# The early sums of a gate-and-up group, made once instead of three times

## The chip, the cores and the metric

The kernel runs on one core of a Trainium2 chip. The metric is the time of one execution on the device in microseconds (us). Lower is better. The engines named below are TensorE (PE, the matmuls, with PEld for its weight loads), VectorE (DVE), ScalarE (ACT), GpSimd (POOL) and SyncE (SP, which issues the weight transfers). Each engine works through its own list of instructions in order and waits on semaphores where an instruction needs another engine's result.

## The reference

The reference is a two-block network in float32 on one sequence of 256 tokens of width 2048. Block one has an attention and retention mixer, a cross attention and a gated feed-forward layer; block two has another mixer and another feed-forward layer. The change touches only the feed-forward layer of block one, with 5632 hidden columns:

```
hf = rmsnorm(x, norm_ffn_g[l])
x = x + (jax.nn.silu(hf @ w_gate[l]) * (hf @ w_up[l])) @ w_down[l]
```

## The kernel before

Every float32 matrix is split into a high and a low part, and a product is made of three matmuls (`mm3`, L193 to L195: high by high, high by low, low by high). The weights stream in from memory as tiles of 128 x 2048 (1 MB each), in the order in which they are used. For each piece of a weight tile, ACT makes the high part by a cast (L175, `wh`) and DVE the low part by a subtraction (L176, `wl`). `half` (L319) hands out the next piece and prepares pieces ahead, so that up to five are in line.

The gate and up weights are computed together in 11 groups of 512 hidden columns, in three parts of 4, 4 and 3 groups (`PARTS`). Behind each part comes its share of the down product. One group is a call of `gemm_q` (L410). It runs 8 passes `u` over the inner dimension, each with 256 rows of the gate weight and 256 of the up weight, for 256 tokens. `KINDS = "NSNSNSNN"` says how each pass is done:

- "S" (passes 1, 3 and 5) is a Strassen step of seven products in place of eight. It needs sums of weight blocks, which DVE makes (L305, L309 and L310, `wt`), and has four pieces "a", "c", "b", "d".
- "N" (passes 0, 2, 4, 6 and 7) is a plain step of eight products with two pieces. The first piece gives two products into M2 and two into M4, the second two into M5 and two into M3.

The products gather in seven accumulators, M1 to M7, of one PSUM bank each. M2 to M5 come from a pool of four banks (`pg` in the profile), M1, M6 and M7 from another pool of four (`pp`). Only "S" passes add to M1, M6 and M7, so these three are complete behind pass 5; M2 to M5 are complete only in pass 7. Since all four `pg` banks are in use, the next group's product into a bank can't begin before the bank's old content has been read.

How the accumulators become gate and up: the early sums are a copy m of M1 (L844, ACT), u2 = M6 + m (L845, DVE) and u3 = M7 + u2 (L846, DVE). They are made by the function `early`, which `gemm_q` calls as `sums_done` at the end of a pass (L448) if no "S" pass is left. That holds behind passes 5, 6 and 7. The second and third call write the same values into the same tiles again. The rest is made when `gemm_q` returns:

- gate, first 128 tokens: M2 + m (L853, DVE, reads M2 for the last time), then silu (L854, ACT)
- gate, last 128 tokens: M4 + u3 (L855, DVE, reads M4 for the last time), then silu (L856, ACT)
- up: M5 + u2 and M5 + u3 (L857 and L858), M3 + that u2 (L859), and the two products with the gate (L861, L860), all on DVE

The order of the instructions on each engine is not written by hand. The framework plans it ahead of the run from a simulated timeline (`schedule_with_timeline_sim=True`), allots the buffers of the pools and puts the semaphores in. An instruction may therefore stand before others that were written earlier: DVE's list mixes weight pieces of the next group with the sums of the present one.

Of the kernel before, what the change touches and what calls it, by code (L numbers as in the profile page):

```python
# [17 lines left out]
S = 256  # L18
# [28 lines left out]
def tile_kernel(ctx, tc, x, xT, mem, memT, par, alibi, rdecay, ident_d, bc_rows, gm_wsT,  # L47
# [98 lines left out]
    def gps():  # L146
        return psg.tile([P, 512], F32, tag="g", name=nm("pg"))

    def sps():
        return pss.tile([P, 512], F32, tag="p", name=nm("pp"))  # L150
# [40 lines left out]
    def mm3(out, lh, rh, start, stop):  # L191

        T.matmul(out, lhsT=lh[0], rhs=rh[0], start=start, stop=False)  # L193
        T.matmul(out, lhsT=lh[0], rhs=rh[1], start=False, stop=False)  # L194
        T.matmul(out, lhsT=lh[1], rhs=rh[0], start=False, stop=stop)  # L195
# [68 lines left out]
    def kind(w, u):  # L264
        return KINDS[u] if w is w_gu else "N"
# [53 lines left out]
    def half(w, g, u, i, n):  # L319
        while pos[1] < len(pieces) and len(feed) < 1 + LOOKAHEAD:  # L320
            push()
        w_, g_, u_, i_, hi, lo = feed.pop(0)
        assert w_ is w and (g_, u_, i_) == (g, u, i)
        if isinstance(hi, list):
            return hi, lo
        return [[t[:, k * n:(k + 1) * n] for k in range(t.shape[-1] // n)] for t in (hi, lo)]
# [4 lines left out]
    def tick():  # L331
        for g in list(bg):
            try:
                next(g)
            except StopIteration:
                bg.remove(g)
# [8 lines left out]
    def need(lst, i):  # L345
        while lst[i] is None:
            assert bg
            tick()
        return lst[i]
# [60 lines left out]
    def gemm_q(wap, g, acts, sums_done):  # L410

        M = [None] * 8
        n = len(acts)
        ks = [kind(wap, u) for u in range(n)]
        total = {m: sum(1 if k == "S" else 2 if m in (2, 3, 4, 5) else 0 for k in ks) for m in range(1, 8)}
        done = [0] * 8

        def prod(m, a, b):  # L420
            if M[m] is None:
                M[m] = gps() if m in (2, 3, 4, 5) else sps()
            done[m] += 1
            mm3(M[m], a, b, done[m] == 1, done[m] == total[m])

        for u in range(n):
            a = need(acts, u)
            if ks[u] == "N":
                plan = [(0, [(2, 0, 0, 0), (2, 0, 1, 1), (4, 1, 0, 0), (4, 1, 1, 1)]),
                        (1, [(5, 1, 1, 0), (5, 1, 0, 1), (3, "D", 1, 0), (3, "D", 0, 1)])]  # L430
                for i, ops in plan:
                    hi, lo = half(wap, g, u, i, 512)
                    for m, t, k, b in ops:
                        prod(m, a.diff(k) if t == "D" else a.blk(k, t), (hi[b], lo[b]))
                    tick()
            else:
                plan = [("a", [(1, a.blk(0, 0), 0), (2, a.blk(1, 0), 1)]),
                        ("c", [(3, a.sums(3), 0)]),
                        ("b", [(5, a.sums(0), 0), (7, a.sums(2), 1)]),
                        ("d", [(6, a.sums(1), 0), (4, a.blk(1, 1), 1)])]  # L440
                for i, ops in plan:
                    hi, lo = half(wap, g, u, i, 512)
                    for m, x, b in ops:
                        prod(m, x, (hi[b], lo[b]))
                    if i in "cd":
                        tick()
            if "S" not in ks[u + 1:]:
                sums_done(M)  # L448
        return M

    def evac_fm(ps, r):
# [386 lines left out]
    for g0, g1 in PARTS:  # L838
        acts = [None] * (2 * (g1 - g0))
        for g in range(g0, g1):  # L840
            m, u2, u3 = flat(ft()), flat(ft()), flat(ft())

            def early(M):
                A.copy(m, M[1])  # L844
                V.tensor_tensor(u2, M[6], m, ALU.add)  # L845
                V.tensor_tensor(u3, M[7], u2, ALU.add)  # L846

            M = gemm_q(w_gu, g, hf_a, early)
            if g == 0:
                rsf[0] = sqf.rstd(D)  # L850
            r = [rsf[0][:, t:t + 1] for t in range(2)]
            s = [flat(ft()), flat(ft())]
            V.tensor_tensor(s[0], M[2], m, ALU.add)  # L853
            A.activation(s[0], s[0], AF.Silu, scale=r[0])  # L854
            V.tensor_tensor(s[1], M[4], u3, ALU.add)  # L855
            A.activation(s[1], s[1], AF.Silu, scale=r[1])  # L856
            V.tensor_tensor(u2, M[5], u2, ALU.add)  # L857
            V.tensor_tensor(u3, M[5], u3, ALU.add)  # L858
            V.tensor_tensor(u2, M[3], u2, ALU.add)  # L859
            V.scalar_tensor_tensor(s[0], u2, r[0], s[0], ALU.mult, ALU.mult)  # L860
            V.scalar_tensor_tensor(s[1], u3, r[1], s[1], ALU.mult, ALU.mult)  # L861
            spawn(ffn_pairs(s, acts, 2 * (g - g0)))
        for g in range(4):
            add_x(gemm_tm(w_down, g, acts, g0), g)
            if g1 == PARTS[-1][1]:
                spawn(next_in(g, h2_a, sq_f, gg, second_norm), 1)
# [218 lines left out]
    for g in range(2):  # L1085
        ps = gemm_tm(w_in2_t, g, h2_a)
        u = []
# [161 lines left out]
```

## Time and profile before

| | us |
|---|---|
| runs, median of 3 (lowest to highest) | 2601.64 (2598.96 to 2602.27) |
| the profiled execution | 2601.45 |
| its span, first to last instruction | 2599.7 |
| gate-and-up groups of part 1 (0 to 3) | about 807 to 962 of the span |
| part 2 (4 to 7) | about 1046 to 1224 |
| part 3 (8 to 10) | about 1308 to 1442 |

Each of the three stretches is followed by a down stage. A row of a group of instructions gives line, engine, operation, tiles (output from inputs, buffer numbers left out), shapes and count, then the busy time in us and the mean of one in ns, then the engine's idle time just before them and what ended it. A row of single instructions gives the start in us from the start of the span, the duration, and in brackets the idle time before it with the instruction that ended it. A row of waits gives who waited for whom: us in total, times, longest. A row of a stretch gives its bounds, its length, the busy time of PE, PEld, DVE, ACT and POOL with instruction counts, the granted clock of PE as a share of full speed, the share of the DMA engines that was busy, and GB/s. A duration on DVE or ACT overlaps the next instruction's by some 0.08 us, so what an instruction takes from a full queue is the step from its start to the next start.

### The profile page before, as it was taken

To read this page: it belongs to the slowest core of one execution; us is meant where nothing else is said; L and a number is where in the kernel's file an instruction comes from. 1 tells how busy PE (TensorE), PEld (TensorE's weight loads), DVE (VectorE), ACT (ScalarE), POOL (GpSimd) and SP (SyncE) were. 2 spreads that over 40 slices of the span, in tenths; PEclk is the share of its full clock that TensorE was granted. 3 is DMA by queue.
4 is the path that set the end of the run, shared out by engine and by line. 5 is a ranking of instruction groups with operands and counts; after the bars stand their busy time and mean duration, and the time that the engine had idled before them with its cause. 6 is when DMAs were issued, how large, how long until landed. Compare 5 with 4: busy or idle time off the path is not lost.

```text
span 2599.7 us, 32474 instructions
## 1 busy us (share of the span) xinstructions
PE 2567.3 (99%) x12823; PEld 2172.7 (84%) x12823; DVE 1789.2 (69%) x2284; ACT 1381.7 (53%) x1882; POOL 39.0 (2%) x41
## 2 busy tenths in 40 slices
PE   8999999999999999999999999999999999999998
PEld 7888888888887878878887888888888888888887
DVE  7666566556579885888588767866777745777754
ACT  6555554454466553555355555755555534555543
POOL 1000010000000000000000000000000000000000
PEclk9999999999999999999999999999999999999999
DMA  7455555554454555455555555555555555555563
GB/s 257 162 179 211 201 201 189 194 178 162 146 188 168 196 193 194 178 206 196 193 182 180 205 208 192 178 192 181 188 185 193 184 193 192 194 185 188 189 213 132
DMA packets 72727, 490.58 MB, mean 189 GB/s; under 512 B 8192, under 2 KB 8320, under 8 KB 14592
## 3 DMA queue, kind: packets, MB, share of 16 engines
q1 hardware_dynamic: 72576, 488.52, 53.1%
q8 instruction: 100, 1.64, 0.2%
q14 instruction: 51, 0.42, 0.0%
HBM read 486.39 MB, written 2.10 MB: 188 GB/s over the span
## 4 chain that ended last, share of the span: by engine, by line
PE 94%; DVE 3%; issue 1%; ACT 1%; DMA 0%; SPq 0%; POOL 0%; ACTq 0%; POOLq 0%; DVEq 0%
PE pg L362 24%; PE pg L193 17%; PE pg L195 17%; PE pg L194 17%; PE pg L366 12%; PE pp L193 2%; PE pp L195 2%; PE pp L194 2%; DVE wl L176 1%; PE pp L186 1%; ACT wh L175 1%; DVE wt L305 0%; DVE f L845 0%; DVE f L846 0%; DMA w<-in_w_in_f_dram 0%
## 5 line engine op out<-in xcount | busy, mean ns | idle before, releaser
L176 DVE TENSOR_TENSOR wl<-w,wh 128x1024 fp32r<-128x1024 f32 x866 | 1059.6, 1225 | 665.7 <-ACT wh L175 662.0
L175 ACT CAST wh<-w 128x1024 fp32r<-128x1024 f32 x866 | 909.2, 1051 | 863.9 <-PE pg L195 583.9
L193 PE MATMUL pg<-wh,r 128*128 128x512 f32 x2059 | 798.6, 392 | 12.7 <-DVE f L855 11.2
L194 PE MATMUL pg<-wl,r 128*128 128x512 f32 x2059 | 804.6, 391 | 0.0
L195 PE MATMUL pg<-wh,r 128*128 128x512 f32 x2059 | 802.3, 390 | 0.0
L362 PE MATMUL pg<-r,wh 128*128 128x512 f32 x2688 | 714.9, 395 | 11.4 <-ACT wh L175 7.0
L362 PEld LDWEIGHTS pg<-r,wh 128*128 128x128 f32 x2688 | 471.0, 189 | 86.2 <-ACT wh L175 7.0
L193 PEld LDWEIGHTS pg<-wh,r 128*128 128x128 f32 x2059 | 387.2, 188 | 98.3 <-DVE f L855 14.7
L195 PEld LDWEIGHTS pg<-wh,r 128*128 128x128 f32 x2059 | 387.6, 188 | 80.7
L194 PEld LDWEIGHTS pg<-wl,r 128*128 128x128 f32 x2059 | 387.8, 188 | 80.4 <-DVE wl L176 1.1
L366 PEld LDWEIGHTS pg<-r,wl 128*128 128x128 f32 x2688 | 391.2, 190 | 41.7
L366 PE MATMUL pg<-r,wl 128*128 128x256 f32 x2688 | 406.0, 282 | 0.0
L454 ACT COPY f<-pg 128x256 f32<-128x256 f32 x168 | 60.7, 374 | 88.7 <-PE pg L362 88.7
L175 ACT CAST wh<-wt 128x1024 fp32r<-128x1024 f32 x66 | 69.6, 1055 | 55.3 <-DVE wt L310 21.2
L455 DVE TENSOR_TENSOR f<-pg,f 128x256 f32<-128x256 f32 x168 | 68.9, 420 | 43.7 <-ACT f L454 43.7
L176 DVE TENSOR_TENSOR wl<-wt,wh 128x1024 fp32r<-128x1024 f32 x66 | 80.3, 1219 | 11.9 <-ACT wh L175 11.2
L1112 DVE SCALAR_TENSOR_TENSOR f<-f,pr,f 128x255 f32<-128x255 f32 x192 | 79.9, 479 | 0.0
L456 DVE TENSOR_TENSOR f<-f,rows 128x512 f32<-128x512 f32 x84 | 58.1, 692 | 3.4 <-ACT rows L231 0.8
L1109 ACT ACTIVATE f<-f,pr 128x256 f32<-128x256 f32 x96 | 52.6, 594 | 12.6 <-DVE f L456 12.5
L175 ACT CAST r<-f 128x512 fp32r<-128x512 f32 (+1 forms) x72 | 43.0, 598 | 13.7 <-DVE f L456 8.7
L193 PE MATMUL pp<-wh,r 128*128 128x512 f32 x127 | 49.6, 395 | 0.0
L195 PE MATMUL pp<-wh,r 128*128 128x512 f32 x127 | 49.5, 390 | 0.0
(192 smaller groups left out, 1354.0 us busy)
## 6 DMA issues: line engine op xcount, KB each, us to landing
w<-in_w_up_dram SPq DMA_DIRECT2D x96, 1024.0 KB, 4.7
w<-in_w_down_dram SPq DMA_DIRECT2D x92, 1024.0 KB, 4.7
w<-in_w_gu_dram SPq DMA_DIRECT2D x88, 1024.0 KB, 4.8
w<-in_w_in_t_dram SPq DMA_DIRECT2D x40, 1024.0 KB, 4.8
w<-in_w_in_f_dram SPq DMA_DIRECT2D x39, 1024.0 KB, 4.7
w<-in_w_o_dram SPq DMA_DIRECT2D x16, 1024.0 KB, 4.8
w<-in_w_xk_dram SPq DMA_DIRECT2D x16, 1024.0 KB, 4.8
w<-in_w_xv_dram SPq DMA_DIRECT2D x16, 1024.0 KB, 4.7
```

Of the source, the lines that this page charges most:

```text
L175: A.copy(hi, src)
L176: V.tensor_tensor(lo, src, hi.bitcast(F32), ALU.subtract)
L193: T.matmul(out, lhsT=lh[0], rhs=rh[0], start=start, stop=False)
L194: T.matmul(out, lhsT=lh[0], rhs=rh[1], start=False, stop=False)
L195: T.matmul(out, lhsT=lh[1], rhs=rh[0], start=False, stop=stop)
L362: T.matmul(ps[m], lhsT=hi[k][:, m * P:(m + 1) * P], rhs=ops[k].both(k % 2), start=begin and k == 0, stop=stop, skip_group_check=True)
L366: T.matmul(ps[m][:, S:], lhsT=lo[k][:, m * P:(m + 1) * P], rhs=ops[k].hi(k % 2), start=False, stop=False, skip_group_check=True)
L454: A.copy(f[:, m, :], ps[m][:, S:])
L455: V.tensor_tensor(f[:, m, :], ps[m][:, 0:S], f[:, m, :], ALU.add)
L456: V.tensor_tensor(f, f, bc2(need(r, 0)), ALU.mult)
L1109: A.activation(y[:, j, :], z[:, j, :], AF.Identity, scale=col("ffn_conv_w_2", 192 + c), bias=col("ffn_conv_b_2", c))
L1112: V.scalar_tensor_tensor(y[:, j, d:], z[:, j, :S - d], col("ffn_conv_w_2", 96 * (2 - d) + c), y[:, j, d:], ALU.mult, ALU.add)
```

## The change

The test for "is an S pass left" and the call move by one level of indentation, into the branch for "S" passes. Behind pass 5 the early sums are made as before; behind passes 6 and 7 ("N") nothing is made.

```
@@ -444,8 +444,8 @@
                         prod(m, x, (hi[b], lo[b]))
                     if i in "cd":
                         tick()
-            if "S" not in ks[u + 1:]:
-                sums_done(M)
+                if "S" not in ks[u + 1:]:
+                    sums_done(M)
         return M
```

`early`, `gemm_q`'s products, the final sums and everything else stay as they are.

More of the change, by code (lines that the diff above doesn't have):

```diff
@@ L446, in gemm_q @@
                         tick()
-            if "S" not in ks[u + 1:]:
-                sums_done(M)
+                if "S" not in ks[u + 1:]:
+                    sums_done(M)
         return M
```

## The prediction

> **What bounds the kernel now.** I read the head of the page first, then the waits of TensorE in the gate-and-up stage, then the stage's stretches, then single instructions around the group boundaries.
>
> ```profile
> span 2599.7 us, 32474 instructions
> PE 2567.3 (99%) x12823; PEld 2172.7 (84%) x12823; DVE 1789.2 (69%) x2284; ACT 1381.7 (53%) x1882; POOL 39.0 (2%) x41
> PE 94%; DVE 3%; issue 1%; ACT 1%; DMA 0%; SPq 0%; POOL 0%; ACTq 0%; POOLq 0%; DVEq 0%
> ```
>
> TensorE (PE) is busy for 2567.3 of 2599.7 us. The whole kernel can give back at most 32.4 us of idle PE, plus whatever PE loses while it counts as busy. The chain that ended last has 3% on VectorE (DVE), about 78 us; the question is whether the removed work is part of that. The waits of PE between 800 and 1450 us, which is gate, up and down, are two rows (total, times, longest):
>
> ```profile
> PE pg L193 <- DVE f L855: 11.2, 4, 3.1
> PE pg L193 <- ACT wh L175: 1.3, 4, 0.3
> ```
>
> Four times PE waits for L855, 2.8 us each. L855 is the addition `M4 + u3`: it releases M4's bank, which the next group's third product needs, and it needs `u3`, which the removed calls rewrite. By stretches (length, then busy time of PE, PEld, DVE, ACT, POOL, then granted clock and DMA):
>
> ```profile
> 807.00:962.00 155.00, 148.80 (x657) 121.53 (x656) 138.14 (x165) 87.29 (x101) 0.00 (x0) 0.99 0.54 191
> 962.00:1046.00 84.00, 84.00 (x376) 69.65 (x375) 46.38 (x45) 35.38 (x36) 0.00 (x0) 1.00 0.57 198
> 1046.00:1224.00 178.00, 174.55 (x775) 142.27 (x774) 157.77 (x180) 99.56 (x113) 0.00 (x0) 1.00 0.53 190
> 1308.00:1442.00 134.00, 130.95 (x569) 106.88 (x569) 115.19 (x131) 74.38 (x84) 0.00 (x0) 0.97 0.52 183
> ```
>
> The first, third and fourth are the gate-and-up groups of the three parts, the second a down stage. In the groups DVE is busy 86 to 89% of the time, in the down stage 55%, where PE is never idle. So DVE's 69% over the span hides a stage where it is nearly full, and PE's idle time is there. Now one boundary on DVE (start, duration; the first row ends the first call of the early sums, the second begins the second):
>
> ```profile
> 902.90 0.68 DVE L846 TENSOR_TENSOR f<-pp,f 128x512 f32<-128x512 f32 x1
> ...
> 904.64 0.68 DVE L845 TENSOR_TENSOR f<-pp,f 128x512 f32<-128x512 f32 x1
> 905.24 1.21 DVE L305 TENSOR_TENSOR wt<-w 128x1024 f32<-128x1024 f32 x1
> ...
> 906.97 0.68 DVE L846 TENSOR_TENSOR f<-pp,f 128x512 f32<-128x512 f32 x1
> 907.57 1.21 DVE L176 TENSOR_TENSOR wl<-w,wh 128x1024 fp32r<-128x1024 f32 x1
> ...
> 910.44 0.68 DVE L853 TENSOR_TENSOR f<-pg,f 128x512 f32<-128x512 f32 x1
> 911.04 0.68 DVE L845 TENSOR_TENSOR f<-pp,f 128x512 f32<-128x512 f32 x1
> 911.64 0.68 DVE L310 TENSOR_TENSOR wt<-wt,w 128x512 f32<-128x512 f32 x1
> 912.24 1.22 DVE L176 TENSOR_TENSOR wl<-wt,wh 128x1024 fp32r<-128x1024 f32 x1
> 913.38 0.68 DVE L846 TENSOR_TENSOR f<-pp,f 128x512 f32<-128x512 f32 x1
> 913.98 1.21 DVE L176 TENSOR_TENSOR wl<-wt,wh 128x1024 fp32r<-128x1024 f32 x1
> 915.11 1.22 DVE L305 TENSOR_TENSOR wt<-w 128x1024 f32<-128x1024 f32 x1
> 916.25 0.68 DVE L855 TENSOR_TENSOR f<-pg,f 128x512 f32<-128x512 f32 x1
> ```
>
> From 904.64 on no row shows idle time: DVE works through its queue without a pause for 12 us, and four of these instructions, the second and third calls, are what the change removes. PE at the same moment:
>
> ```profile
> 913.65 0.39 PE L194 MATMUL pg<-wl,r 128*128 128x512 f32 x1
> 913.88 0.39 PE L195 MATMUL pg<-wh,r 128*128 128x512 f32 x1
> 916.98 0.50 PE L193 MATMUL pg<-wh,r 128*128 128x512 f32 x1 [2.71 <-DVE f L855]
> ```
>
> Matmuls follow at 0.23 us, so the next was due at 914.11 and came at 916.98. Before the stall the new group had run its two products into M2.
>
> **The change, part by part.** The rows of the three lines over the whole run:
>
> ```profile
> L844 ACT COPY f<-pp 128x512 f32<-128x512 f32 x33 | 19.1, 577 | 0.1
> L845 DVE TENSOR_TENSOR f<-pp,f 128x512 f32<-128x512 f32 x33 | 22.6, 684 | 1.0 <-PE pp L195 0.7
> L846 DVE TENSOR_TENSOR f<-pp,f 128x512 f32<-128x512 f32 x33 | 22.5, 683 | 0.0
> ```
>
> 33 is three for each of 11 groups; one is left. (That the change leaves the repeats in place can't be: the call now stands in the branch for "S", and only pass 5 has no "S" behind it.) Removed are 22 copies of 0.58 us on ScalarE (ACT), 12.7 us, and 44 additions on DVE. Their occupancy is the step from start to start, 904.64 to 905.24, 0.60 us: 26.4 us of DVE, 2.40 us per group.
>
> *The four long stalls.* If the order on DVE stays and the queue closes up, L855 starts at 916.25 - 2.40 = 913.85. PE resumed 0.73 us behind L855's start, so at 914.58 against 914.11 due: 0.47 us late instead of 2.87. That needs the weight halves from ACT in time:
>
> ```profile
> 909.55 1.06 ACT L175 CAST wh<-wt 128x1024 fp32r<-128x1024 f32 x1 [1.66 <-PE pg L195]
> 911.16 0.73 ACT L854 ACTIVATE f<-f,s 128x512 f32<-128x512 f32 x1 [0.56 <-DVE f L853]
> 912.41 1.05 ACT L175 CAST wh<-wt 128x1024 fp32r<-128x1024 f32 x1 [0.53 <-DVE wt L310]
> 916.96 0.72 ACT L856 ACTIVATE f<-f,s 128x512 f32<-128x512 f32 x1 [3.50 <-DVE f L855]
> ```
>
> The cast of 912.41 feeds the L176 of 913.98. It follows L854, whose earliest start is the end of the cast of 909.55, near 910.5; so it runs from about 911.2 to 912.2, 0.6 us later than the closed-up DVE would want it (913.98 - 2.40 = 911.6), and the stall is 1.1 us. The other bound is none: at the boundary before, L855 has only one weight piece behind L846.
>
> ```profile
> 868.13 0.68 DVE L846 TENSOR_TENSOR f<-pp,f 128x512 f32<-128x512 f32 x1
> 868.73 1.21 DVE L176 TENSOR_TENSOR wl<-wt,wh 128x1024 fp32r<-128x1024 f32 x1
> 869.86 0.68 DVE L855 TENSOR_TENSOR f<-pg,f 128x512 f32<-128x512 f32 x1
> 870.46 0.68 DVE L857 TENSOR_TENSOR f<-pg,f 128x512 f32<-128x512 f32 x1
> ```
>
> In both patterns L853 stands at the same place among the weight pieces, and L855 comes behind the third L846. I read that as L855 queueing three times (L845, L846, itself) behind weight pieces that were ready first. With `u3` made long before, it needs only M4 and should move up towards L853. Between 0 and 1.1 us I take 0.3 left at each: 11.2 - 4 x 0.3 = **10.0 us** gained.
>
> *The slow matmuls behind two of them.* Stretches behind the first, second and fourth stall:
>
> ```profile
> 826.26:830.50 4.24, 4.24 (x12) 3.33 (x13) 4.24 (x8) 1.75 (x2) 0.00 (x0) 0.60 0.00 0
> 917.00:922.00 5.00, 5.00 (x22) 4.16 (x23) 5.00 (x8) 1.74 (x2) 0.00 (x0) 1.00 0.00 0
> 1397.60:1404.00 6.40, 6.38 (x15) 4.98 (x16) 5.42 (x8) 1.76 (x2) 0.00 (x0) 0.52 0.01 3
> ```
>
> The granted clock is 0.60 and 0.52 there and 1.00 behind the second. Lost: 4.24 x 0.40 = 1.7 and 6.40 x 0.48 = 3.1, together **4.8 us**, which count as busy. The four short stalls are 0.3 us at most, and the stretch from 1046 to 1224, which holds one long and two short ones, has 1.00; so I expect no slow stretch behind a short stall and take all of it as gained; the bound is none of it.
>
> [...]
>
> *The four short stalls*, 1.3 us, wait for a cast. ACT works in order and stands at L856 until L855 is done (the 3.50 above), with the next cast behind it. An earlier L855 lets it go; between 0 and 1.3 I take half, **0.6 us**.
>
> *Nothing else is on the path.* The copies go from an ACT that is 53% busy; its casts wait for PE to free buffers, and that cover gone each copy would cost 0.58 us. The banks of M1, M6 and M7 are released with the first call (L846 of 902.90 rather than 913.38), but PE has no wait on them: 0. No wait and no DMA is added, and no DMA moves past another. Next in line to be late is weight traffic: the groups run at a DMA share of 0.54, with room. The planner orders the whole kernel anew; outside this stage there is hardly a PE wait to move, so I allow 2 us either way.
>
> **Sum**: 10.0 + 4.8 + 0.6 = 15.4 us from the profiled execution's 2601.45 us (its span and 1.75 us around it; the median of the runs is 2601.64): **2586.0 us**. Bounds: all of the three terms, 17.3, and 2 of drift give 2582; none gives 2601.
>
> **The rivals.**
>
> *The queue fills up again: no change, 2601.* The planner puts weight pieces ahead of L855: the L305 of 915.11 belongs to products that run 16 us later, and still it goes first. If the freed 2.40 us takes in two more L176 (1.13 us each from start to start), 0.14 us per boundary is left, 0.6 in all, and the stalls keep their lengths: 2601. For it: L855's delay is an order fixed before the run. Against: the weight pieces wait for buffers that PE frees (the 1.66 <-PE above), so there are few to pull forward.
>
> [...]
>
> *Every boundary becomes a long one: slower.* The four short ones differ from the long ones by one L305 ahead of L855. If the new plan places L176 and L305 between L853 and L855 everywhere and pulls one more piece in, all eight stall for 2.8 us: 4 x (2.8 - 0.3) = 10 us more, and with half of them followed by a slow stretch of 2.4 us, as now, 4.8 more: 2616. It decides from three weight pieces (3.4 us) between L853 and L855, since PE needs M4 only two products after the group starts. For it: two of eight boundaries already differ in order without any difference in the code. Against: there is less work on DVE, and `u3` can only be ready sooner.
>
> *Only the closed-up queue, clock unchanged.* Order kept, stalls of 1.1 us left, and the slow stretches stay: 11.2 - 4.4 = 6.8 us, 2594.6.
>
> **How the numbers follow.** Forecast 0.64, partial gain 0.10, no change 0.15, slower 0.11. About 0.2%, 5.2 us, is what a measurement of this kernel can tell from no change: faster (below 2596.4) has the first two, 0.74, same 0.15, slower 0.11. The range goes from 2581, everything gained with the drift, to 2600, which takes in the partial case and a part of "no change", and leaves out slower and the rest, some 0.2. The forecast's own range is 2581 to 2592.
>
> **What would show it.** L844, L845 and L846 at 11 each. The row of PE waiting for L855 falls from 11.2 us to under 2. L855 starts within two weight pieces of L853 at all eight boundaries. The granted clock is 1.00 throughout the three group stretches, and these shorten by 5 us or so each while the down stages keep 84.0. DVE's share in the groups falls only slightly, since they get shorter too. I am wrong if PE's wait moves to another line of the group's end (L857 to L859, or a cast) with the same sum, or if L855 keeps two L176 and an L305 ahead of it and the stall stays above 2 us.

## The result

The changed kernel takes 2579.59 us (median of 4 runs, 2579.35 to 2579.97), the kernel before 2601.95 us (4 runs, 2598.96 to 2604.46). The ratio is 0.9915, with a 95% interval from 0.9897 to 0.9932: 22.4 us faster. The forecast was 2586.0 us in a range from 2581 to 2600. The direction and the place were right; the gain was half again as large as forecast, and the time lies 1.4 us below the range.

The head of the page of the changed kernel, its chain that ended last, and all waits of PE in the whole run (total, times, longest):

```profile
span 2577.7 us, 32402 instructions
PE 2558.0 (99%) x12823; PEld 2171.4 (84%) x12823; DVE 1764.1 (68%) x2240; ACT 1369.3 (53%) x1860; POOL 40.6 (2%) x41
PE 98%; issue 0%; DVE 0%; ACT 0%; DMA 0%; POOL 0%; SPq 0%; ACTq 0%; POOLq 0%; DVEq 0%
```

```profile
PE pg L362 <- ACT wh L175: 7.0, 1, 7.0
PE pg L362 <- DVE r L179: 3.8, 4, 1.5
PE pg L362 <- DVE f L455: 0.5, 2, 0.3
```

DVE is gone from the chain (3% before). None of the three rows left is a gate-and-up wait: 7.0 and 3.8 us are the start of the kernel. The stretches of the three parts' groups (same columns as before) have no idle PE and full clock:

```profile
807.00:952.00 145.00, 145.00 (x653) 120.33 (x652) 127.96 (x149) 82.57 (x93) 0.00 (x0) 1.00 0.57 203
1058.00:1210.00 152.00, 152.00 (x685) 126.09 (x684) 131.41 (x145) 84.34 (x94) 0.00 (x0) 1.00 0.56 202
1310.00:1423.00 113.00, 113.00 (x508) 93.76 (x507) 96.86 (x106) 62.38 (x69) 0.00 (x0) 1.00 0.57 205
```

DVE is still 86 to 88% busy there. It has the same share of a shorter stage; its share alone would not have told that the stall is gone. How much shorter the stage is can be read from the first early copy and the last product of up and gate (count, durations in ns, first and last start). Of the kernel before:

```profile
L844 ACT COPY f<-pp x33: 567/578/589, 807.2 to 1434.0; 128x512 f32<-128x512 f32 x33
L860 DVE SCALAR_TENSOR_TENSOR f<-f,s,f x11: 741/744/747, 829.8 to 1444.5; 128x512 f32<-128x512 f32 x11
```

Of the changed kernel:

```profile
L844 ACT COPY f<-pp x11: 580/581/589, 807.3 to 1405.0; 128x512 f32<-128x512 f32 x11
L860 DVE SCALAR_TENSOR_TENSOR f<-f,s,f x11: 740/744/745, 827.7 to 1422.3; 128x512 f32<-128x512 f32 x11
```

The stage starts at the same time and ends 22.2 us earlier; the span is 22.0 us shorter. All of the gain is made here. The same boundary as in the prediction, on DVE of the changed kernel:

```profile
896.64 0.68 DVE L846 TENSOR_TENSOR f<-pp,f 128x512 f32<-128x512 f32 x1
897.24 1.21 DVE L176 TENSOR_TENSOR wl<-w,wh 128x1024 fp32r<-128x1024 f32 x1
898.38 1.22 DVE L305 TENSOR_TENSOR wt<-w 128x1024 f32<-128x1024 f32 x1
...
901.85 1.22 DVE L176 TENSOR_TENSOR wl<-w,wh 128x1024 fp32r<-128x1024 f32 x1
902.99 0.68 DVE L853 TENSOR_TENSOR f<-pg,f 128x512 f32<-128x512 f32 x1
903.59 0.68 DVE L310 TENSOR_TENSOR wt<-wt,w 128x512 f32<-128x512 f32 x1
904.19 0.68 DVE L855 TENSOR_TENSOR f<-pg,f 128x512 f32<-128x512 f32 x1
904.79 1.22 DVE L176 TENSOR_TENSOR wl<-wt,wh 128x1024 fp32r<-128x1024 f32 x1
```

L855 now comes one short piece behind L853, as the prediction expected once u3 was early; before, six instructions lay between them. The first L855 of each kernel (the first start is the one at the first boundary, up to which both run alike), before and then after:

```profile
L855 DVE TENSOR_TENSOR f<-pg,f x11: 679/682/687, 825.5 to 1439.1; 128x512 f32<-128x512 f32 x11
```

```profile
L855 DVE TENSOR_TENSOR f<-pg,f x11: 679/681/684, 819.5 to 1416.6; 128x512 f32<-128x512 f32 x11
```

It moved by 6.0 us (825.52 to 819.55): 2.4 us are the four removed additions, 3.4 us are two L176 and an L305 that now stand behind it. PE needs M4 there at about 823.0 (826.26, where it came, less its delay of 3.25 us). L855 with its 0.7 us was 3.2 us late before and is 2.8 us early now.

**What the sum had missed.** The short boundary at 870 us, on PE of the kernel before:

```profile
870.15 0.39 PE L195 MATMUL pg<-wh,r 128*128 128x512 f32 x1
870.60 0.50 PE L193 MATMUL pg<-wh,r 128*128 128x512 f32 x1
870.93 0.39 PE L194 MATMUL pg<-wl,r 128*128 128x512 f32 x1
...
872.33 0.50 PE L194 MATMUL pg<-wl,r 128*128 128x512 f32 x1
872.66 0.40 PE L195 MATMUL pg<-wh,r 128*128 128x512 f32 x1
873.39 1.17 PE L193 MATMUL pg<-wh,r 128*128 128x512 f32 x3 [0.34 <-ACT wh L175]
874.40 0.39 PE L194 MATMUL pg<-wl,r 128*128 128x512 f32 x1
```

The idle time is 0.34 us, which is what the wait row counts. But 870.15 to 870.60, 872.33 to 872.66, 872.66 to 873.39 and the three L193 in 1.0 us are all longer than the usual 0.23 us from start to start. Nearly all of this counts as busy in the profile (PE 4.20 of the 4.60 us from 870.40 to 875.00). Adding up every step above 0.26 us from 780 to 1450 us of the span, less the usual 0.2265 us each, gives 22.8 us in 70 steps before and 1.3 us in 15 steps after: 16.8 us at the four long boundaries with their slow stretches, 4.9 us at the four short ones, and about 1.1 us in single steps of 0.31 us that both kernels have. So the stage held 21.5 us to gain, and all of it was gained.

What PE waited for at a short boundary shows in its weight loads (PEld), which run 0.23 us ahead of the matmuls here (the load for the L194 of 870.93 began at 870.70). The same boundary, the four loads that waited:

```profile
870.60 0.19 PEld L193 LDWEIGHTS pg<-wh,r 128*128 128x128 f32 x1 [0.48 <-DVE f L855]
872.33 0.19 PEld L194 LDWEIGHTS pg<-wl,r 128*128 128x128 f32 x1 [0.27 <-DVE wl L176]
873.39 0.30 PEld L193 LDWEIGHTS pg<-wh,r 128*128 128x128 f32 x2 [0.77 <-ACT wh L175]
874.06 0.19 PEld L193 LDWEIGHTS pg<-wh,r 128*128 128x128 f32 x1 [0.37 <-DVE f L858]
```

So a short boundary is not one wait for a cast but four waits, the first for L855 and the last for M5's last sum, L858; PE's own rows count a part of the third alone. The other three short boundaries show the same four. In the changed kernel no weight load of the stage waits.

### The profile page after: what moved, and what is told of

Its sections match the earlier page's. It is cut to its first block, busy times and chain, and to the rows that moved or that the text cites. A ratio compares the mean times of both kernels' runs of the same rounds, so it can differ in the third digit from the quotient of the medians.

```text
span 2577.7 us, 32402 instructions
## 1 busy us (share of the span) xinstructions
PE 2558.0 (99%) x12823; PEld 2171.4 (84%) x12823; DVE 1764.1 (68%) x2240; ACT 1369.3 (53%) x1860; POOL 40.6 (2%) x41
## 4 chain that ended last, share of the span: by engine, by line
PE 98%; issue 0%; DVE 0%; ACT 0%; DMA 0%; POOL 0%; SPq 0%; ACTq 0%; POOLq 0%; DVEq 0%
PE pg L362 24%; PE pg L193 18%; PE pg L195 18%; PE pg L194 18%; PE pg L366 12%; PE pp L195 2%; PE pp L194 2%; PE pp L193 2%; PE pp L186 1%; DMA w<-in_w_in_f_dram 0%; DVE r L179 0%; DVE wl L176 0%; PE pp L945 0%; PE pp L997 0%; PE pp L998 0%
## 5 line engine op out<-in xcount | busy, mean ns | idle before, releaser
L176 DVE TENSOR_TENSOR wl<-w,wh 128x1024 fp32r<-128x1024 f32 x866 | 1059.7, 1225 | 666.8 <-ACT wh L175 662.8
L194 PE MATMUL pg<-wl,r 128*128 128x512 f32 x2059 | 802.3, 390 | 0.0
L195 PE MATMUL pg<-wh,r 128*128 128x512 f32 x2059 | 800.9, 390 | 0.0
L193 PE MATMUL pg<-wh,r 128*128 128x512 f32 x2059 | 794.3, 390 | 0.0
L362 PE MATMUL pg<-r,wh 128*128 128x512 f32 x2688 | 714.8, 395 | 11.4 <-ACT wh L175 7.0
L195 PEld LDWEIGHTS pg<-wh,r 128*128 128x128 f32 x2059 | 386.5, 188 | 80.2
L194 PEld LDWEIGHTS pg<-wl,r 128*128 128x128 f32 x2059 | 386.6, 188 | 79.6
L193 PEld LDWEIGHTS pg<-wh,r 128*128 128x128 f32 x2059 | 386.6, 188 | 79.1
L176 DVE TENSOR_TENSOR wl<-wt,wh 128x1024 fp32r<-128x1024 f32 x66 | 80.4, 1219 | 10.4 <-ACT wh L175 9.8
L1109 ACT ACTIVATE f<-f,pr 128x256 f32<-128x256 f32 x96 | 52.5, 595 | 12.6 <-DVE f L456 12.5
L193 PE MATMUL pp<-wh,r 128*128 128x512 f32 x127 | 49.7, 395 | 0.0
L195 PE MATMUL pp<-wh,r 128*128 128x512 f32 x127 | 49.5, 390 | 0.0
```

What stands on the lines that cost most here:

```text
L176: V.tensor_tensor(lo, src, hi.bitcast(F32), ALU.subtract)
L362: T.matmul(ps[m], lhsT=hi[k][:, m * P:(m + 1) * P], rhs=ops[k].both(k % 2), start=begin and k == 0, stop=stop, skip_group_check=True)
L1109: A.activation(y[:, j, :], z[:, j, :], AF.Identity, scale=col("ffn_conv_w_2", 192 + c), bias=col("ffn_conv_b_2", c))
```

## The experiments

The question was what made L855 late. One theory, "queueing", says the chain of repeated calls: each call must wait for the one before it (same tiles), each addition stands in line behind weight pieces, and L855 comes behind the last u3. The rival, "load", says DVE's time: 2.4 us more in a full queue.

**One repeat instead of two.** On the changed kernel:

```
-                if "S" not in ks[u + 1:]:
-                    sums_done(M)
+            if u in (5, 6):
+                sums_done(M)
```

> The early sums are made twice, behind passes 5 and 6; half of the removed work is back (1.2 us of VectorE per group). Theory 'queueing' (the last repeat makes u3 late, and L855 stands in line three times behind weight pieces): with one repeat the last u3 is made well before M4 is complete, L855 directly follows L853, so PE never waits for it and the time is that of the changed kernel, 2580 +-2 us. Theory 'load' (what counts is VectorE's queue time, 2.4 us per group): half of the stall is back, 4 x 1.2 us and one or two slow stretches, 2585 to 2591 us.

Measured: 2580.11 us (ratio to the kernel before 0.9918, 0.9903 to 0.9933), no PE wait in the stage. Half of the removed work costs 0.5 us, not half of 22. L853 and L855 stand next to each other (904.77 and 905.37). This speaks against a price per microsecond of load, but does not yet show that the chain of repeated calls is what counts.

**The same work without the chain.** The repeats write to spare tiles, which L853 to L859 don't read:

```
+            spare = [flat(ft()) for _ in range(3)]
-            def early(M):
-                A.copy(m, M[1])
+            def early(M, u):
+                a, b, c = (m, u2, u3) if u == 5 else spare
+                A.copy(a, M[1])
...
+            if u in (5, 6, 7):
+                sums_done(M, u)
```

> All three calls as before, but those behind passes 6 and 7 write into three spare tiles that nothing reads: the same 22 copies and 44 additions, the same reads of M1, M6 and M7, without L855 and its like depending on them. 'Queueing': no PE wait for the sum into s[1], time 2580 to 2583 us. 'Load': as the kernel before, 2595 to 2602 us, with four stalls of 2 to 3 us.

Measured: 2587.18 us (0.9945, 0.9930 to 0.9959). Neither theory: some 14 us of the 22 are gained, 7.6 us are not. No wait for the sums is left; PE waits six times 0.9 us for a cast (PE of this run; the piece's other matmuls follow):

```profile
911.09 0.39 PE L195 MATMUL pg<-wh,r 128*128 128x512 f32 x1
911.32 0.39 PE L193 MATMUL pg<-wh,r 128*128 128x512 f32 x1
912.62 0.72 PE L193 MATMUL pg<-wh,r 128*128 128x512 f32 x2 [0.91 <-ACT wh L175]
```

Here an L193 follows an L193, where usually L194 and L195 come between. I read that as a matmul of the next weight piece that the planner put ahead of its turn, as at the short boundaries of the kernel before. That piece's cast waited for PE to free a buffer (ACT of this run):

```profile
911.52 1.04 ACT L175 CAST wh<-w 128x1024 fp32r<-128x1024 f32 x1 [1.57 <-PE pg L195]
```

Whether a sixth buffer for the high parts would remove this stays open: the kernel with six did not fit into on-chip memory (a pool of 6.5 kB per partition would have had 4.25 kB), so there is no time for it.

**The same, each repeat twice.** `sums_done` is called twice behind passes 6 and 7, into the same spare tiles.

> As the run with spare tiles, with each repeated call made twice: four calls more per group than the changed kernel, 8 additions or 4.8 us of VectorE on top of its 37.6 us of 42.4 us per group, so VectorE is full. 'Queueing' with a limit: now VectorE sets the pace and PE waits appear, for weight pieces rather than for the sum; 0 to 2 us per group, 2582 to 2602 us. 'Load': clearly slower than the kernel before, above 2605 us, since twice its extra load is there.

Measured: 2588.08 us (0.9950, 0.9933 to 0.9966). Twice the extra load costs 0.9 us more. PE now waits 2.6 us in three times for M5's last sum (L858, here L861) and 2.6 us in three times for a cast. "Load" is out as a price per microsecond.

**A set of spare tiles for each repeat.** `spare[u - 6]` in place of `spare`: now no call waits for another.

> Again 22 more copies and 44 more additions than the changed kernel, but each repeated call has a set of spare tiles of its own, so that no call waits for the one before it. If lateness in the chain of calls is what costs, and VectorE's 2.4 us per group fit into its slack of 4.8 us: 2580 to 2582 us and no PE wait in the stage. If the 7.6 us of the run with one shared set of spare tiles are the price of the load itself: 2586 to 2588 us again.

Measured: 2589.51 us (0.9955, 0.9940 to 0.9970). The chain is quite gone, and the time is 2.3 us worse than with one shared set. Here PE waits for M2's sum, which is L855 in this file, two lines further down:

```profile
PE pg L193 <- DVE f L855: 7.1, 8, 2.1
```

Free to run, the spare additions come sooner and stand ahead of that sum. So part of the price is plain queue time in front of the sums.

**The chain with nearly no work.** The kernel before, but the second and third call remake 8 of 512 columns:

```
+            def early(M, n):
+                A.copy(m[:, :n], M[1][:, :n])
+                V.tensor_tensor(u2[:, :n], M[6][:, :n], m[:, :n], ALU.add)
+                V.tensor_tensor(u3[:, :n], M[7][:, :n], u2[:, :n], ALU.add)
...
+            if u in (5, 6, 7):
+                sums_done(M, 512 if u == 5 else 8)
```

> The kernel before with all three calls into the same tiles, but the calls behind passes 6 and 7 make only the first 8 of 512 columns again: the chain of dependences on L855 stays, nearly all of VectorE's load goes. If the chain alone costs the rest that the runs with spare tiles did not show (12 to 14 us): 2590 to 2595 us. If the additions can queue without harm once they are short (each waits behind weight pieces as before, but takes 0.15 us): 2580 to 2586 us.

Measured: 2581.16 us (0.9917, 0.9902 to 0.9932); PE waits once, 0.4 us. L855 still stands behind the third call and a weight piece:

```profile
903.84 0.69 DVE L853 TENSOR_TENSOR f<-pg,f 128x512 f32<-128x512 f32 x1
904.44 0.69 DVE L310 TENSOR_TENSOR wt<-wt,w 128x512 f32<-128x512 f32 x1
905.04 0.16 DVE L846 TENSOR_TENSOR f<-pp,f 128x8 f32<-128x8 f32 x1
905.12 1.22 DVE L176 TENSOR_TENSOR wl<-wt,wh 128x1024 fp32r<-128x1024 f32 x1
906.25 0.69 DVE L855 TENSOR_TENSOR f<-pg,f 128x512 f32<-128x512 f32 x1
```

But everything ahead of it is 2.1 us shorter, and it is in time. The chain with nearly no work costs 1.6 us, not 12. These short calls also take the work off ACT's copies, so the run does not tell DVE's additions from ACT's copies.

**The same DVE time at two places.** On the changed kernel, four additions of 128x512 per group that nothing reads, on the low weight parts of one pass (2 in one run, 7 in the other):

```
                     hi, lo = half(wap, g, u, i, 512)
+                    for _ in range(2 if u == 2 else 0):
+                        V.tensor_tensor(spare, lo[0].bitcast(F32), lo[1].bitcast(F32), ALU.add)
```

> The changed kernel with four additions of 128x512 per group that nothing reads, on the low weight parts of pass 2: 2.4 us of VectorE per group as in the runs with spare tiles, but in the middle of the group. If the total load counts (7.6 to 9.9 us in those runs): 2587 to 2590 us. If only VectorE's queue at the group's end counts: 2580 to 2582 us and no PE wait.

> The same four additions on the low weight parts of pass 7, so that they stand in VectorE's queue ahead of L853 and L855. Queue at the group's end: 2586 to 2590 us, with PE waiting for the sums or a cast by about 1 us at most boundaries. Total load: the same as with pass 2. If neither costs: 2580 us.

Measured: pass 2, 2580.09 us (0.9914, 0.9897 to 0.9930); pass 7, 2582.47 us (0.9924, 0.9909 to 0.9938). One group's stretch with the load in pass 2:

```profile
828.60:871.00 42.40, 42.40 (x193) 35.20 (x192) 39.81 (x51) 23.82 (x27) 0.00 (x0) 1.00 0.55 199
```

DVE is 94% busy, and PE loses nothing. At the group's end the same work costs 2.4 us more, less than the 6 to 10 us that I had expected. Three of the four additions stand ahead of M2's and M4's sums there, and both still come in time: PE has no wait in the stage. Its weight loads have one, for M5's last sum (L858, here L860), which is about what was lost:

```profile
PEld pg L193 <- DVE f L860: 2.6, 6, 0.5
```

**A fourth call.** The kernel before with two calls behind pass 7:

```
             if "S" not in ks[u + 1:]:
-                sums_done(M)
+                for _ in range(2 if u == 7 else 1):
+                    sums_done(M)
```

> The kernel before with a fourth call of the early sums, made twice behind pass 7, into the same tiles. 'Queueing': the last u3 stands in line two more times; L855 moves back by 2 x 0.60 us of additions and one or two weight pieces between them, some 2.5 to 4 us per boundary; all eight boundaries stall for 3 to 6 us, and most of them are followed by a slow stretch of 2 to 3 us, since the idle time is longer: 2620 to 2650 us. 'Load': 1.2 us per group more than before, 2605 to 2614 us.

Measured: 2625.74 us (ratio 1.0094, 1.0077 to 1.0111). All eight boundaries stall, twice each (L854 and L856 are M2's and M4's sums, one line further down in this file):

```profile
PE pg L193 <- DVE f L856: 18.2, 8, 2.3
PE pg L193 <- DVE f L854: 12.4, 8, 2.0
```

So one, two, three and four calls give 2580, 2580, 2602 and 2626 us. The first repeat is nearly free, and each further one costs 22 to 24 us, part of it in slow stretches behind the stalls (the last section).

**Using the room.** The changed kernel with a fourth Strassen pass per group, `KINDS = "NSSNSNSN"`:

> The changed kernel with KINDS = NSSNSNSN: a fourth Strassen pass per group, one product of three matmuls less (0.68 us of PE, 7.5 us in 11 groups), and some 4 us more of VectorE per group (three sums of weight blocks, and four pieces in place of two), 41.6 of 41.7 us. If VectorE's slack of 4.8 us per group is real and usable: 2572 to 2576 us, faster than both. If bunching eats it: PE waits for weight pieces, 2580 to 2600 us.

Measured: 2593.4 us (0.9970, 0.9959 to 0.9982), 13.8 us slower than the changed kernel. PE waits for M2's sum and for casts:

```profile
PE pg L193 <- DVE f L853: 8.8, 8, 2.9
PE pg L193 <- ACT wh L175: 2.4, 6, 0.7
```

The sums come late again, and more is lost than the 7.5 us of matmuls saved. Why is not shown. DVE is 93 to 95% busy in two groups of this run, but it was 94% busy in the run with the load in pass 2, which lost nothing. The edit also makes pass 6 an "S" pass, so that the early sums come one pass later; the run with calls behind passes 5 and 6 suggests that this alone costs little. In the next run its L305 goes to GpSimd (`G.tensor_tensor` in place of `V.tensor_tensor`):

> The changed kernel with four Strassen passes, as in the run e6, and the wide subtraction of weight blocks (L305, four of 1.14 us per group) moved from VectorE to GpSimd, which is idle in this stage. VectorE falls to some 37 us of 41.7 us per group, so PE should no longer wait for L853: 2572 to 2576 us. A 128x512 addition took GpSimd 1.55 us in the kernel before, so this one should take some 3 us, four times in 41.7 us; if it slows VectorE beside it or comes late for the cast, 2580 to 2600 us.

Measured: 2606.64 us (1.0020, 1.0010 to 1.0030), slower still. GpSimd and DVE of this run:

```profile
896.84 3.78 POOL L305 TENSOR_TENSOR wt<-w 128x1024 f32<-128x1024 f32 x1 [9.40 <-DMA w<-in_w_gu_dram]
```

```profile
898.34 3.36 DVE L176 TENSOR_TENSOR wl<-w,wh 128x1024 fp32r<-128x1024 f32 x1
```

The DVE subtraction, 1.22 us elsewhere, took 3.36 us and ended at 901.70, GpSimd's instruction at 900.62. From 807 to 1445 us of this run DVE's 271 wide L176 took 363.2 us, 32.6 us above 1.22 us each, and its 41 narrow ones on weights (`r` from `w`) 39.4 us, 11.4 us above the 0.684 us of the changed kernel. The L305 of this stretch (41, as many as L309) would have taken some 46 us of DVE's list at 1.13 us each, an estimate. So most of what left the list came back as longer subtractions on DVE. None of these runs is faster than the changed kernel.

## Why the prediction was right and where it was wrong

- *Place and cause*: right. The waits for L855 and the short ones are gone, L844 to L846 stand at 11 each, the down stages and all else are as they were.
- *"L855 queueing three times"*: right as to the order (L855 next to L853 with the third call gone), half right as a cause. The chain with nearly no work costs 1.6 us, the work without the chain 7.6 to 9.9 us at the same passes, both together 22. A picture that fits is a room of 2.8 us between the end of M4's sum and PE's need: one repeat stays within it, and the second goes 3.2 us beyond. That is argued from the rows, and it is not the whole: the runs with spare tiles lost their time at other places, at a cast (5.5 us), at M5's sum (2.6 us) and at M2's sum (7.1 us), whose rooms were not measured.
- *The four long stalls* (10.0 us) *and the slow stretches* (4.8 us): 14.8 us forecast, 16.8 us by matmul spacing, all gained. The 0.3 us that I left at each long boundary was 0; the other 0.8 us PE lost around the stalls while it counted as busy. The slow stretches themselves were sized rightly (1.7 and 3.0 us by spacing).
- *The four short stalls*: the step that failed. I read one wait for a cast, sized it from PE's idle time, 1.3 us in all, and took half, with no row behind the half. There were four waits at each, for L855, a low part, the cast and L858; by matmul spacing they cost 4.9 us, and all of it went. This alone is 4.3 of the 6.6 us missing from the sum (22.0 us of span against 15.4), the long stalls are 2.0, and 0.3 I can't place. It is also why the lower end of the range was too high: my bound of "all three terms, 17.3 us" was built from idle time and the two slow stretches, and leaves out what PE loses at full clock while it counts as busy. With 2 us of drift it gave 2582.2, and the range took 2581.
- *The clock*: right to count the two stretches at 0.60 and 0.52 as lost time; in the changed kernel the three parts' stretches have 1.00. In 29 timed runs of the kernel before, its spread goes with the mean granted clock: 2604.0 us on average at 0.996 (9 runs), 2601.9 at 0.997 (8), 2599.7 at 0.998 (12). A step of 0.001 of 2600 us is 2.6 us; found are 2.1 and 2.2. The changed kernel had 0.999 in all four runs, 0.6 us apart.
- *The rivals*: "the queue fills up again" did not happen; the freed time was not taken by weight pieces ahead of L855. "Every boundary becomes a long one" came about only with a fourth call. "Order kept, clock unchanged" did not happen.
- *Copies on ACT, earlier release of M1, M6 and M7*: nothing showed a price or a gain of their own, but no run changed the copies alone.

What stays open: why 44 more additions cost 0.5, 2.9, 7.6 or 9.9 us. The runs with 7.6 and 9.9 us also have the 22 copies on ACT and read PSUM, the other two have no copies and read low weight parts, so they differ in more than the place. The planner rearranges PE's list too (the matmul put ahead of its turn, above), and no run held that order fixed.

## What to carry to other kernels

Here work that DVE did twice was nearly free as long as the consumer's deadline left room, and cost 22 us from the point where it didn't; so look at how early the value is when it is needed, not at the engine's share of busy time (86 to 89% here both with and without the stalls). Size a stall by the distance from matmul to matmul against the usual one, not by idle time alone: here 22.8 us against 12.5 us of idle; the waits of the weight loads tell what for. Rewriting a tile with the same values is not harmless for its readers: here L855 stood behind the last of three writers of `u3`, and that order with nearly no work cost 1.6 us, with the work 22.

## What the runs showed of the hardware that was not expected

The clock was low behind two of the kernel before's long stalls, the first (0.60) and the last (0.52), and 1.00 behind the two between them. PE's rows at the first, third and last, and the stretch behind the third:

```profile
826.26 0.50 PE L193 MATMUL pg<-wh,r 128*128 128x512 f32 x1 [3.09 <-DVE f L855]
1135.45 0.50 PE L193 MATMUL pg<-wh,r 128*128 128x512 f32 x1 [2.71 <-DVE f L855]
1397.62 0.79 PE L193 MATMUL pg<-wh,r 128*128 128x512 f32 x1 [2.71 <-DVE f L855]
```

```profile
1135.40:1140.00 4.60, 4.55 (x20) 3.78 (x21) 4.60 (x8) 1.78 (x2) 0.00 (x0) 1.00 0.00 2
```

It was low behind shorter stalls too. In the run with a set of spare tiles per call no wait of PE in the stage was longer than 2.1 us, and this stretch at the first boundary has 0.62; in the run with four calls none was longer than 2.3 us, and these two have 0.64:

```profile
823.52:828.00 4.48, 4.48 (x13) 3.53 (x14) 4.48 (x7) 2.54 (x3) 0.00 (x0) 0.62 0.37 155
```

```profile
877.90:882.60 4.70, 4.66 (x13) 3.68 (x14) 4.70 (x7) 1.77 (x2) 0.00 (x0) 0.64 0.00 0
926.30:931.00 4.70, 4.62 (x13) 3.72 (x14) 4.46 (x8) 1.77 (x2) 0.00 (x0) 0.64 0.00 0
```

In the latter PE waits twice at each boundary, 1.55 us on average for M2's sum and 2.28 us for M4's. Two stalls of 2.71 us in the kernel before were followed by no slow stretch, one was; so length alone does not decide, and what does stays open.

Beside a GpSimd subtraction (L305, 896.84 to 900.62 us in the run with it on GpSimd) a DVE subtraction took 3.36 us, 2.1 us more than the usual 1.22. GpSimd's instruction was long as well, 3.78 us against 2.41 us in the median of 44. Another DVE subtraction, at 897.67 and thus beside it too, took its usual 0.68 us. So both instructions of this pair were slow side by side, but not every DVE instruction there was; which of the two held up the other, and by what, no run shows.
